# A transformer block on one core: the down product's tiles laid over the up operands in the order of their last reads, and its sums moved to VectorE

## The chip, the core and the metric

The kernel runs on one NeuronCore of a Trainium2 chip. Its engines work side by side from queues of their own: TensorE (PE) multiplies, VectorE (DVE), ScalarE (ACT) and GpSimd (POOL) do element-wise work, SyncE (SP) mostly issues DMA transfers. The metric is the device time of one execution in microseconds.

## The reference

One layer of a hybrid encoder, 1024 tokens by 1024 features in float32: two attentions, a gated merge, an output projection, and a feed-forward part. The change touches only the last part:

```python
    x = x + merged @ w_out[l]
    h2 = rms_norm(x, norm2[l])
    x = x + jnp.square(jax.nn.relu(h2 @ w_up[l])) @ w_down[l]
return rms_norm(x, final_norm)
```

`w_up` is 1024 x 4096, `w_down` 4096 x 1024.

## The kernel before

Every large product is a Strassen product of 2 x 2 blocks: seven block products in place of eight, named by their weight operand A11, S1, S2, S3, S4, A12, A22, each with an activation operand B11, T1, T2, T3, B22, B21, T4 (sums and differences of blocks). Each factor is split in a high and a low part (`wh`, `wl` of a weight, `xh`, `xl` of an operand), and each product is three matmuls: high by high, low by high, high by low. ACT casts the high part (L148 for weights, L251 for operands); the low part is a subtraction, on POOL for weights (L150) and on DVE for operands (L252).

*Up.* Sixteen units `u` run all seven products in the order A11, S2, S1, S3, A12, S4, A22, twelve matmuls each, with the seven operands held in SBUF in `xop`. DVE combines the banks (L481 to L493), applies relu and the norm (L820), ACT squares, and the results are stored as the seven operands of down in `a_dram`.

*Down.* The outer loop runs over the seven products in the order of `STEPS` (A11, S1, S2, S3, S4, A12, A22), the inner one over 16 steps `k`, with twelve matmuls a step into four PSUM banks `dA` or `dS`. `prepare` runs three steps ahead (`LEAD`): it loads an operand tile from `a_dram` (tile `xr`, transfers called xB or xT, six buffers), splits it (`xB11h`, `xT1l` and so on, four buffers each), and makes the weight. The weight tiles are `ka` (A11's, kept and turned into S3's in place, later loaded anew) and `ks` (S1's, then S2's, then S4's, in place), 16 each; quarters that are only passing are `wr`.

Sums: `p1`, `u`, `v`, `w` (in the profile `accp`, `accu`, `accv`, `accw`), four tiles of 128 x 512 each, gather the products. `evacuate` empties the four banks at the end of a product, `between` is a generator that is stepped once per step of the next product; `residual` loads a tile `r` of the layer's input to the feed-forward part and adds it; `final` squares and scales for the last norm.

Where tiles lie: pools are stacked from the left and the right end of SBUF. `operands` opens a pool for each named operand of up, 16 KB per partition each, on the left, and at the end of up they are closed, and down's pools take their place from the left on. A tile of down waits until the tile that lay there before has been read for the last time. The instructions of each engine are then put in order by a scheduler, so the text of the code gives dependencies and priorities and not the final order.

Of the kernel before, what the change touches and what calls it, by code (L numbers as in the profile page):

```python
# [14 lines left out]
ALU = mybir.AluOpType  # L15
# [56 lines left out]
def hs(h):  # L72
    return slice(h * HALF, (h + 1) * HALF)
# [3 lines left out]
def hybrid_block(ctx: ExitStack, tc: tile.TileContext, xT, g1, wall, wf, fb, relb, relt, rows, g2, g3, outT):  # L77
    nc = tc.nc
    V, A, G, T = nc.vector, nc.scalar, nc.gpsimd, nc.tensor
# [4 lines left out]
    def pool(stack, name, side, bufs=1, **kw):  # L84
        return stack.enter_context(tc.tile_pool(name=name, bufs=bufs, side=side, reuse_waits="tile", **kw))
# [9 lines left out]
    def tmp(name, dt=F32):  # L95
        return tp.tile([P, HALF], dt, tag="t", name=name, bufs=8)
# [9 lines left out]
    for n, (step, cm) in enumerate(((-1, 1), (1, -1))):  # L106
        m = cpool.tile([P, 3, P], F32R, tag=f"mask{n}", name=f"mask{n}")
# [180 lines left out]
    for h in range(2):  # L288
        banks = [psd[1 - h].tile([P, HALF], F32, tag="d", name=f"g{c}_{h}") for c in range(EARLY_GATES)]
# [423 lines left out]
    rest, steps = load_rest(*heads[0]), iter(())  # L713
    for n, hd in enumerate(heads):
        sk, more = rest, iter(())
        if n < 15:
            rest = load_rest(*heads[n + 1])
# [31 lines left out]
    for j in range(4):  # L749
        for h in range(2):  # L750
            t = tmp("olt")
            load(t, o_dram[j, :, hs(h)])
            split((oh[:, j, hs(h)], ol[:, j, hs(h)]), t, V)
    for c in range(8):
        for h in range(2):
            m = tmp("m")
# [10 lines left out]
    def operands(*keys):  # L767
        for n in keys:
            p = pool(hstack, "h" + n, "left")
            xop[n] = tuple(p.tile([P, 4, HALF], F32R, tag=n + s, name=n + s) for s in "hl")  # L770

    operands("B11", "B21")
    accs = accs2 = [rstd[:, hs(h)] for h in range(2)]
    held = {}
    for h in range(2):
        if h == 1:
            operands("T2", "T1", "T3", "B22", "T4")
        for n, c in enumerate(PAIRED):
            k = c % 4
            g = gt[:, 1, c:c + 1]  # L780
            w = plain_w(U_OUT + n // 2, n % 2)
            xr = tmp("xr2")
            load(xr, xT[:, c, hs(h)])
            ps = dense(psm[n % 2], f"o{c}_{h}", w, [(mop[h][0][:, kk, :], mop[h][1][:, kk, :]) for kk in range(KC)])
            V.tensor_tensor(xr, ps, xr, op=ALU.add)  # L785
            store(x2_dram[:, c, hs(h)], xr)
            sum_squares(xr, n == 0, accs[h], V if h else G)
            xg = tmp("xg")
            V.tensor_scalar(xg, xr, g, None, op0=ALU.mult)  # L789
            if h == 0:  # L790
                key = "B11" if c < 4 else "B21"
                split((xop[key][0][:, k, :], xop[key][1][:, k, :]), xg, V)
                continue
            old = tmp("xo")
            load(old, x2_dram[:, c, hs(0)])
            A.activation(old, old, AF.Copy, scale=g)
            held[c] = (old, xg)
            if c >= 4:
                split((xop["B22"][0][:, k, :], xop["B22"][1][:, k, :]), xg, V)
                combine(xop, k, *held[k], *held[c], (V, V))  # L800
        mstack[h].close()
# [39 lines left out]
    def sums(*names):  # L841
        p = pool(ctx, "acc" + names[0], "left")
        for n in names:
            acc[n] = p.tile([P, 4, HALF], F32, tag="acc" + n, name="acc" + n)

    held = {}
    sums("p1", "u")
    hp = {"a": pool(ctx, "ka", "left"), "s": pool(ctx, "ks", "left")}
    sums("v", "w")
    xr = pool(ctx, "xr", "right")  # L850

    def hold(t, k):
        held[t, k] = hp[t].tile([P, HALF], F32, tag=t, name=f"k{t}{k}", bufs=16)
# [23 lines left out]
    p1, au, av, aw = [acc[n] for n in ("p1", "u", "v", "w")]  # L877

    def residual(dst, m, row, h, src, eng):

        r = tmp(f"r{m}_{row}_{h}")
        load(r, x2_dram[:, m + 4 * row, hs(h)])
        eng.tensor_tensor(dst[:, m, :], src[:, m, :], r, op=ALU.add)

    def final(dst, m, row, h):

        dst = dst[:, m, :]
        sum_squares(dst, h not in begun, accs[h], V)
        begun.add(h)
        A.activation(dst, dst, AF.Copy, scale=gt[:, 2, m + 4 * row:m + 4 * row + 1])  # L890
# [17 lines left out]
                n += 1  # L908
                yield

    def evacuate(n, m, bank):
        at = lambda t: t[:, m, :]
        if n in ("A11", "S1"):
            A.copy(at({"A11": p1, "S1": av}[n]), bank)
        elif n == "S2":
            V.tensor_tensor(at(au), bank, at(p1), op=ALU.add)
        else:
            for t in {"S3": (aw, au), "S4": (av,), "A12": (p1,), "A22": (au,)}[n]:
                V.tensor_tensor(at(t), bank, at(t), op=ALU.add)

    def between(n):

        for m in range(4):
            at = lambda t: t[:, m, :]
            if n == "S2":
                V.tensor_tensor(at(av), at(av), at(au), op=ALU.add)
                residual(aw, m, 1, 1, av, V)
                yield
                residual(au, m, 1, 0, au, G)
            elif n == "S3":  # L930
                residual(av, m, 0, 1, av, G)
                yield
                final(aw, m, 1, 1)
            elif n == "S4":
                residual(p1, m, 0, 0, p1, G)
                final(av, m, 0, 1)
            elif n == "A12":
                final(p1, m, 0, 0)
            elif n == "A22":
                final(au, m, 1, 0)  # L940
            yield
        if n == "S4":
            yield
            yield from finish(psm[0], 1, (av, aw), (V, G))
        elif n == "A22":
            yield from finish(psm[1], 0, (p1, au), (V, V, G))
# [10 lines left out]
    ready, rest = [], iter(())  # L957
    for s, (i, n, x, k) in enumerate(steps):
        while len(ready) < min(s + LEAD + 1, len(steps)):
            ready.append(prepare(*steps[len(ready)][1:]))  # L960
        if k == 0:
            banks = [psm[i % 2].tile([P, HALF], F32, tag="d", name=f"d{n}_{m}") for m in range(4)]
        xs, wh, wl = ready[s]
        for m in range(4):
            product(banks[m], k == 0, [((wh[:, m, :], wl[:, m, :]), xs)], k < 15)
        if k:
            next(rest, None)
        if k == 15:
            for m in range(4):
                evacuate(n, m, banks[m])  # L970
            rest = between(n)
    for _ in rest:
        pass

# [61 lines left out]
```

## Time and profile before

| what | us |
|---|---|
| runs | 1597.46, 1597.52, 1600.31; median 1597.52 |
| profiled execution | 1596.17, its span 1594.4, mean granted clock 0.969 |
| TensorE busy | 1476.5 (93%) |
| DVE, ACT, POOL busy | 1051.9 (66%), 741.5 (47%), 964.5 (60%) |
| up's last matmul to down's first, from the span's start | 1240.1 to 1257.2 |
| down's seven products | 1257.2 to 1574.9 |
| after the last matmul of down | some 20 |

In a group's row the numbers are the count, then durations in ns. In a timeline's row they are the start and the duration in us, then the engine, the line, the operation, output and inputs, and in brackets how long the engine had been idle before it and what ended that. SPq is SyncE's queue of transfers. In a row of waits: total, times, longest.

### The profile page before, as it was taken

To read this page: it belongs to the slowest core of one execution; us is meant where nothing else is said; L and a number is where in the kernel's file an instruction comes from. 1 tells how busy PE (TensorE), PEld (TensorE's weight loads), DVE (VectorE), ACT (ScalarE), POOL (GpSimd) and SP (SyncE) were. 2 spreads that over 40 slices of the span, in tenths; PEclk is the share of its full clock that TensorE was granted. 3 is DMA by queue.
4 is the path that set the end of the run, shared out by engine and by line. 5 is a ranking of instruction groups with operands and counts; after the bars stand their busy time and mean duration, and the time that the engine had idled before them with its cause. 6 is when DMAs were issued, how large, how long until landed. Compare 5 with 4: busy or idle time off the path is not lost.

```text
span 1594.4 us, 21236 instructions
## 1 busy us (share of the span) xinstructions
PE 1476.5 (93%) x6788; PEld 1213.0 (76%) x6788; DVE 1051.9 (66%) x1552; ACT 741.5 (47%) x1391; POOL 964.5 (60%) x746
## 2 busy tenths in 40 slices
PE   6798999999979899999999879999999599989996
PEld 4586888888858788888777758888888488868885
DVE  8988555644457687765414887666666588677763
ACT  5543333343348787657324544333333344435552
POOL 6886777778742232111199648888886355466661
PEclk9899999999979999999999979999999799999998
DMA  4155666873487878874566544444445965444371
GB/s 152 48 146 138 189 195 200 219 206 121 163 192 169 175 161 206 206 204 108 193 210 197 187 145 165 159 151 154 151 152 173 336 218 165 129 142 132 115 226 56
DMA packets 154288, 269.21 MB, mean 169 GB/s; under 512 B 22264, under 2 KB 39928, under 8 KB 151040
## 3 DMA queue, kind: packets, MB, share of 16 engines
q1 hardware_dynamic: 82880, 149.37, 31.3%
q10 hardware_dynamic: 50304, 84.24, 16.5%
q0 software_dynamic: 20992, 34.25, 9.9%
q8 instruction: 53, 0.87, 0.2%
q14 instruction: 59, 0.48, 0.1%
HBM read 181.48 MB, written 86.31 MB: 168 GB/s over the span
## 4 chain that ended last, share of the span: by engine, by line
PE 36%; DMA 6%; DVE 5%; issue 2%; POOL 1%; ACT 1%; SPq 0%; ACTq 0%; DVEq 0%; POOLq 0%
PE u L201 18%; PE dS L201 9%; PE dA L201 6%; DMA wr<-wall 2%; PE o L201 1%; DMA ka<-wall 1%; PE m L201 1%; DMA olt<-o_dram 1%; DMA xr<-xT 1%; POOL wl L150 0%; POOL ml L252 0%; POOL m L759 0%; DVE xr L785 0%; DVE xg L789 0%; DVE ks L866 0%
## 5 line engine op out<-in xcount | busy, mean ns | idle before, releaser
L150 POOL TENSOR_TENSOR wl_A<-wr,wh_A 128x512 fp32r<-128x512 f32 x121 | 174.6, 1447 | 64.1 <-ACT wh_A L148 54.8
L150 POOL TENSOR_TENSOR wl_S<-S,wh_S 128x512 fp32r<-128x512 f32 x105 | 153.0, 1461 | 33.0 <-ACT wh_S L148 30.9
L148 ACT CAST wh_A<-wr 128x512 fp32r<-128x512 f32 x121 | 75.0, 620 | 116.7 <-DMA a_dram<-at 28.1
L252 DVE TENSOR_TENSOR tl<-p,th 128x512 fp32r<-128x512 f32 (+1 forms) x192 | 108.6, 587 | 28.6 <-ACT th L251 23.7
L150 POOL TENSOR_TENSOR wl_S<-ks,wh_S 128x512 fp32r<-128x512 f32 x48 | 68.7, 1434 | 56.1 <-ACT wh_S L148 53.6
L251 ACT CAST th<-p 128x512 fp32r<-128x512 f32 (+1 forms) x192 | 92.4, 509 | 10.3 <-PE pv L676 4.4
L434 DVE CUSTOM_DVE_ANT_0 s<-s,bc 128x384 f32<-128x384 f32 (+3 forms) x128 | 69.7, 562 | 38.5 <-PE s L427 24.1
L148 ACT CAST wh_S<-S 128x512 fp32r<-128x512 f32 x105 | 63.8, 618 | 63.7 <-POOL S L173 27.2
L493 DVE TENSOR_TENSOR cc<-u,u 128x512 f32<-128x512 f32 x70 | 48.0, 686 | 61.1 <-PE u L201 61.0
L427 PE MATMUL s<-qk 128*128 128x384 f32 (+2 forms) x192 | 63.1, 362 | 22.7 <-DMA qk<-qk_dram 15.4
L171 POOL TENSOR_TENSOR S<-wr,wr 128x512 f32<-128x512 f32 x36 | 51.5, 1432 | 53.0 <-DMA wr<-wall 46.7
L150 POOL TENSOR_TENSOR wl_A<-ka,wh_A 128x512 fp32r<-128x512 f32 x32 | 45.6, 1431 | 53.1 <-ACT wh_A L148 53.1
L821 ACT ACTIVATE v<-v 128x512 f32<-128x512 f32 x64 | 40.4, 631 | 69.3 <-DVE v L820 69.1
L660 PE MATMUL st<-sk 82*128 82x512 f32 (+1 forms) x192 | 66.1, 345 | 2.1 <-DMA sk<-m_rows 2.1
L652 PE MATMUL st<-qk 128*128 128x512 f32 (+1 forms) x192 | 66.6, 351 | 0.6 <-ACT p L672 0.5
L675 PE MATMUL pv<-th,v 128*128 128x512 f32 (+1 forms) x192 | 65.6, 342 | 1.0 <-ACT on L688 0.6
L677 PE MATMUL pv<-tl,v 128*128 128x512 f32 (+1 forms) x192 | 65.0, 339 | 0.1
L676 PE MATMUL pv<-th,v 128*64 128x512 f32 (+1 forms) x192 | 64.7, 337 | 0.0
L672 ACT ACTIVATE p<-st,ncq 128x512 f32<-128x512 f32 (+1 forms) x96 | 54.3, 598 | 22.1 <-PE st L668 15.5
L251 ACT CAST qkh<-qk 128x512 fp32r<-128x512 f32 x32 | 19.9, 622 | 95.2 <-DMA qk_dram<-qkl 46.0
L148 ACT CAST wh_S<-ks 128x512 fp32r<-128x512 f32 x48 | 29.8, 621 | 67.8 <-PE dS L201 59.4
L427 PEld LDWEIGHTS s<-qk 128*128 128x128 f32 x192 | 36.2, 199 | 31.4 <-DMA qk<-qk_dram 8.8
(369 smaller groups left out, 5180.4 us busy)
## 6 DMA issues: line engine op xcount, KB each, us to landing
wr<-wall SPq DMA_DIRECT2D x259, 256.0 KB
qk<-qk_dram POOLq DMA_DIRECT2D x16, 1024.0 KB, 6.3
a_dram<-at ACTq DMA_DIRECT2D x64, 256.0 KB
xT<-a_dram SPq DMA_DIRECT2D x64, 256.0 KB
qk_dram<-qkh ACTq DMA_DIRECT2D x96, 128.0 KB
a_dram<-v ACTq DMA_DIRECT2D x48, 256.0 KB
xB<-a_dram SPq DMA_DIRECT2D x48, 256.0 KB
z_dram<-zt ACTq DMA_DIRECT2D x32, 256.0 KB
```

Source lines behind the costliest of these rows:

```text
L148: A.copy(wh, src)
L150: G.tensor_tensor(wl, src, wh.bitcast(F32), op=ALU.subtract)
L201: T.matmul(bank, w[wi], x[xi], start=(first and t == 0), stop=(t == n - 1 and not part), skip_group_check=part or not first)
L251: A.copy(dst[0], src)
L252: eng.tensor_tensor(dst[1], src, dst[0].bitcast(F32), op=ALU.subtract)
L427: T.matmul(ps[:, :n], qk[:, 1, i * P:(i + 1) * P], qk[:, 0, ks:ks + n], start=True, stop=not diag)
L434: V.tensor_tensor_reduce(ps[:, :v], ps[:, :v], bc[:, b0:b0 + v], 1.0, prev, ALU.add, ALU.min, out)
L652: T.matmul(ps[:, c], qk[:, 0, keys], qk[:, 1, qs], start=True, stop=False)
L660: T.matmul(ps[:, c], sk[:, 0, keys], sk[:, 1, qs], start=False, stop=not extra)
L675: T.matmul(pv[:, c], v3[hh][:, j, 1:3, :], th[:, c], start=first, stop=False)
L676: T.matmul(pv[0:HD, c], v3[hh][:, j, 0, :], th[:, c], start=False, stop=False)
L677: T.matmul(pv[:, c], v3[hh][:, j, 1:3, :], tl[:, c], start=False, stop=last)
```

## The change

Three edits.

1. Up's operands are laid out from the left as B11, T2, T1, T3, B21, B22, T4, the order in which a unit reads them (before: B11, B21, T2, T1, T3, B22, T4). Five pools are now opened before the first half of the output projection and two before the second; before it was two and five.
2. Down's pools take their place as `xq` (split operands), `xr` (raw operands), `ka`, the sums `p1` and `u`, `ks`, the sums `v` and `w`, all on the left. Before it was `xq`, `p1` and `u`, `ka`, `ks`, `v` and `w`, with `xr` on the right, where up's epilogue tiles had been. So `xq` lies over B11 in both; `xr` now lies over T2, `ka` over T2 to T3 and `ks` over B21 to T4.
3. `evacuate` is gone. `between` reads the banks itself, one instruction or two per step, and all residuals are on DVE. The grouping of the sums is another one: residuals of `u`, `w` and `v` are added after S1 (with A11's sum added to `v`), `p1`'s after S2, and S2's bank is then added to `u`, `v` and `w` straight from PSUM. Before, `u` took S2's bank, `v` took `u`, and `w` took `v` with its residual. The loop runs out a generator that is left over at a product's end before it starts the next.

```diff
-    operands("B11", "B21")
+    operands("B11", "T2", "T1", "T3", "B21")
...
         if h == 1:
-            operands("T2", "T1", "T3", "B22", "T4")
+            operands("B22", "T4")
...
+    xr = pool(ctx, "xr", "left")
+    hp = {"a": pool(ctx, "ka", "left")}
     sums("p1", "u")
-    hp = {"a": pool(ctx, "ka", "left"), "s": pool(ctx, "ks", "left")}
+    hp["s"] = pool(ctx, "ks", "left")
     sums("v", "w")
-    xr = pool(ctx, "xr", "right")
...
-    def evacuate(n, m, bank):
-        at = lambda t: t[:, m, :]
-        if n in ("A11", "S1"):
-            A.copy(at({"A11": p1, "S1": av}[n]), bank)
-        elif n == "S2":
-            V.tensor_tensor(at(au), bank, at(p1), op=ALU.add)
-        else:
-            for t in {"S3": (aw, au), "S4": (av,), "A12": (p1,), "A22": (au,)}[n]:
-                V.tensor_tensor(at(t), bank, at(t), op=ALU.add)
-
-    def between(n):
+    def between(n, banks):
 
         for m in range(4):
             at = lambda t: t[:, m, :]
-            if n == "S2":
-                V.tensor_tensor(at(av), at(av), at(au), op=ALU.add)
+            add = lambda t, src: V.tensor_tensor(at(t), src, at(t), op=ALU.add)
+            bank = banks[m]
+            if n == "A11":
+                A.copy(at(p1), bank)
+            elif n == "S1":
+                A.copy(at(av), bank)
+                residual(au, m, 1, 0, p1, V)
+                yield
+                add(av, at(p1))
+                yield
                 residual(aw, m, 1, 1, av, V)
                 yield
-                residual(au, m, 1, 0, au, G)
+                residual(av, m, 0, 1, av, V)
+            elif n == "S2":
+                for t in (au, av, aw):
+                    add(t, bank)
+                    yield
+                residual(p1, m, 0, 0, p1, V)
             elif n == "S3":
-                residual(av, m, 0, 1, av, G)
+                add(aw, bank)
+                yield
+                add(au, bank)
                 yield
                 final(aw, m, 1, 1)
-            elif n == "S4":
-                residual(p1, m, 0, 0, p1, G)
-                final(av, m, 0, 1)
...
+            else:
+                t, row, h = {"S4": (av, 0, 1), "A12": (p1, 0, 0), "A22": (au, 1, 0)}[n]
+                add(t, bank)
+                final(t, m, row, h)
...
         if k == 15:
-            for m in range(4):
-                evacuate(n, m, banks[m])
-            rest = between(n)
+            for _ in rest:
+                pass
+            rest = between(n, banks)
```

How the scheduled instructions move, at three places.

SP's queue at the change from up to down. `wr` are weight quarters, `ka` down's first weights, `xB` its first operand tiles (the number tells tiles apart). Before, from the last of 16 ka transfers on:

```order
L860 DMA ka_12701<-wall 128x512
L143 DMA wr_3_12782<-wall 128x512
L143 DMA wr_2_12784<-wall 128x512
L143 DMA wr_3_12814<-wall 128x512
L143 DMA wr_2_12816<-wall 128x512
L143 DMA wr_3_12846<-wall 128x512
L143 DMA wr_2_12848<-wall 128x512
L143 DMA wr_3_12874<-wall 128x512
L143 DMA wr_2_12876<-wall 128x512
L950 DMA xB_12367<-a_dram 128x512
L950 DMA xB_12379<-a_dram 128x512
```

The same queue now, from the last of up's rows on:

```order
L143 DMA wr_2_12756<-wall 128x512
L953 DMA xB_12367<-a_dram 128x512
L953 DMA xB_12379<-a_dram 128x512
L953 DMA xB_12391<-a_dram 128x512
L953 DMA xB_12403<-a_dram 128x512
L953 DMA xB_12431<-a_dram 128x512
L953 DMA xB_12455<-a_dram 128x512
L953 DMA xB_12479<-a_dram 128x512
L953 DMA xB_12503<-a_dram 128x512
L861 DMA ka_12373<-wall 128x512
L861 DMA ka_12385<-wall 128x512
```

Eight operand tiles moved from behind the 16 ka and 8 wr to ahead of them.

DVE at the start of S2 (operand T2). Before, from S1's last rows on:

```order
L870 TENSOR_TENSOR ka_12701<-ka_12701,wr_3_13968 128x512
L252 TENSOR_TENSOR xT1l_13122<-xT_13119,xT1h_13121 128x512
L252 TENSOR_TENSOR xT1l_13150<-xT_13147,xT1h_13149 128x512
L252 TENSOR_TENSOR xT2l_13178<-xT_13175,xT2h_13177 128x512
L252 TENSOR_TENSOR xT2l_13201<-xT_13198,xT2h_13200 128x512
L252 TENSOR_TENSOR xT2l_13224<-xT_13221,xT2h_13223 128x512
L252 TENSOR_TENSOR xT2l_13251<-xT_13248,xT2h_13250 128x512
```

The same place now, from the third low part on:

```order
L252 TENSOR_TENSOR xT2l_13224<-xT_13221,xT2h_13223 128x512
L916 TENSOR_TENSOR accv<-accp_12357,accv 128x512 x2
L884 TENSOR_TENSOR accw<-accv,r_1_1_13345 128x512
L916 TENSOR_TENSOR accv<-accp_12357,accv 128x512
L884 TENSOR_TENSOR accw<-accv,r_1_1_13448 128x512
L884 TENSOR_TENSOR accv<-accv,r_0_1_13371 128x512
L252 TENSOR_TENSOR xT2l_13247<-xT_13244,xT2h_13246 128x512
L916 TENSOR_TENSOR accv<-accp_12357,accv 128x512
L884 TENSOR_TENSOR accw<-accv,r_1_1_13551 128x512
L884 TENSOR_TENSOR accv<-accv,r_0_1_13474 128x512
L884 TENSOR_TENSOR accp_12357<-accp_12357,r_0_0_13798 128x512
L252 TENSOR_TENSOR xT2l_13274<-xT_13271,xT2h_13273 128x512
```

Where S2's low parts had followed each other, additions of two SBUF tiles now stand between the third and the fourth, the fourth and the fifth, and so on to the seventh (4, then 2, after these rows).

DVE at the start of S3 (operand T3), as S2's banks `dS` are emptied. Before:

```order
L873 TENSOR_TENSOR ks_12781<-ka_14043,ks_12781 128x512
L916 TENSOR_TENSOR accu<-dS_0_13259,accp_12351 128x512
L252 TENSOR_TENSOR xT3l_13604<-xT_13601,xT3h_13603 128x512
L916 TENSOR_TENSOR accu<-dS_1_13260,accp_12351 128x512
L926 TENSOR_TENSOR accv<-accv,accu 128x512
L873 TENSOR_TENSOR ks_12813<-ka_14076,ks_12813 128x512
L916 TENSOR_TENSOR accu<-dS_2_13261,accp_12351 128x512
L916 TENSOR_TENSOR accu<-dS_3_13262,accp_12351 128x512
L926 TENSOR_TENSOR accv<-accv,accu 128x512
L883 TENSOR_TENSOR accw<-accv,r_1_1_13685 128x512
L252 TENSOR_TENSOR xT3l_13633<-xT_13630,xT3h_13632 128x512
```

Now, from the third low part (`xT3l`) to the fourth:

```order
L252 TENSOR_TENSOR xT3l_13638<-xT_13635,xT3h_13637 128x512
L916 TENSOR_TENSOR accu<-dS_1_13256,accu 128x512
L916 TENSOR_TENSOR accv<-dS_1_13256,accv 128x512
L916 TENSOR_TENSOR accw<-dS_1_13256,accw 128x512
L874 TENSOR_TENSOR ks_12809<-ka_14100,ks_12809 128x512
L916 TENSOR_TENSOR accu<-dS_2_13257,accu 128x512
L916 TENSOR_TENSOR accv<-dS_2_13257,accv 128x512
L916 TENSOR_TENSOR accw<-dS_2_13257,accw 128x512
L916 TENSOR_TENSOR accu<-dS_3_13258,accu 128x512
L916 TENSOR_TENSOR accv<-dS_3_13258,accv 128x512
L916 TENSOR_TENSOR accw<-dS_3_13258,accw 128x512
L252 TENSOR_TENSOR xT3l_13669<-xT_13666,xT3h_13668 128x512
```

The three additions of bank 0 stand ahead of these rows. Every addition here now reads a bank; those of two SBUF tiles (L926, L883) have left the place.

More of the change, by code (lines that the diff above doesn't have):

```diff
@@ L909, in finish @@
                 yield
-    def evacuate(n, m, bank):
-        at = lambda t: t[:, m, :]
-        if n in ("A11", "S1"):
-            A.copy(at({"A11": p1, "S1": av}[n]), bank)
-        elif n == "S2":
-            V.tensor_tensor(at(au), bank, at(p1), op=ALU.add)
-        else:
-            for t in {"S3": (aw, au), "S4": (av,), "A12": (p1,), "A22": (au,)}[n]:
-                V.tensor_tensor(at(t), bank, at(t), op=ALU.add)
-    def between(n):
+    def between(n, banks):
         for m in range(4):
             at = lambda t: t[:, m, :]
-            if n == "S2":
-                V.tensor_tensor(at(av), at(av), at(au), op=ALU.add)
+            add = lambda t, src: V.tensor_tensor(at(t), src, at(t), op=ALU.add)
[8 more added lines that the diff above has]
+                yield
                 residual(aw, m, 1, 1, av, V)
                 yield
-                residual(au, m, 1, 0, au, G)
+                residual(av, m, 0, 1, av, V)
[4 more added lines that the diff above has]
+                residual(p1, m, 0, 0, p1, V)
             elif n == "S3":
-                residual(av, m, 0, 1, av, G)
+                add(aw, bank)
+                yield
+                add(au, bank)
                 yield
                 final(aw, m, 1, 1)
-            elif n == "S4":
-                residual(p1, m, 0, 0, p1, G)
-                final(av, m, 0, 1)
[L937 to L940, printed above, removed]
+            else:
+                t, row, h = {"S4": (av, 0, 1), "A12": (p1, 0, 0), "A22": (au, 1, 0)}[n]
+                add(t, bank)
+                final(t, m, row, h)
             yield
```

## The prediction

> **What bounds the kernel now.** I first read the busy time stage by stage, cut at the seven products of the down matmul (from, to; PE; PEld; DVE; ACT; POOL; clock; DMA share; GB/s).
>
> ```profile
> 1257.20:1302.90 45.70, 45.50 (x192) 37.21 (x193) 31.33 (x36) 20.24 (x36) 21.16 (x15) 0.96 0.80 263
> 1302.90:1347.20 44.30, 44.30 (x193) 35.70 (x192) 42.91 (x42) 20.16 (x37) 23.27 (x17) 1.00 0.56 175
> 1347.20:1390.90 43.70, 43.70 (x194) 36.19 (x194) 23.33 (x20) 19.05 (x34) 20.68 (x16) 1.00 0.40 121
> 1390.90:1443.90 53.00, 46.41 (x193) 37.48 (x192) 42.72 (x44) 18.97 (x34) 33.37 (x22) 0.94 0.51 153
> 1443.90:1487.60 43.70, 43.70 (x195) 36.18 (x194) 30.50 (x28) 23.13 (x41) 27.88 (x19) 1.00 0.41 120
> 1487.60:1531.10 43.50, 43.50 (x201) 36.22 (x200) 31.84 (x33) 22.31 (x41) 32.77 (x22) 1.00 0.54 170
> 1531.10:1574.90 43.80, 43.80 (x194) 36.25 (x194) 21.98 (x22) 18.86 (x33) 15.78 (x12) 1.00 0.35 109
> ```
>
> They are A11, S1, S2, S3, S4, A12, A22. TensorE alone needs 43.7 for a product, 2.72 for each of its 16 steps; three products take just that. A11 is 2.0 over, S1 0.6, S3 9.3. Then the waits of TensorE, and its rows at the three holes:
>
> ```profile
> PE dA L201 <- ACT xB11h L251: 16.8, 1, 16.8
> PE dS L201 <- DVE xT3l L252: 6.6, 2, 3.7
> 1240.09 0.39 PE L201 MATMUL u<-T4h,wl_A 128*128 128x512 f32 x1
> 1257.24 2.07 PE L201 MATMUL dA<-xB11h,wh_A 128*128 128x512 f32 x4 [16.76 <-ACT xB11h L251]
> 1405.86 0.50 PE L201 MATMUL dS<-xT3l,wh_S 128*128 128x512 f32 x1 [2.92 <-DVE xT3l L252]
> 1406.20 0.40 PE L201 MATMUL dS<-xT3h,wl_S 128*128 128x512 f32 x1
> 1412.58 0.80 PE L201 MATMUL dS<-xT3l,wh_S 128*128 128x512 f32 x1 [3.67 <-DVE xT3l L252]
> 1413.60 0.63 PE L201 MATMUL dS<-xT3l,wh_S 128*128 128x512 f32 x1
> ```
>
> Up's last matmul and down's first lie 16.8 us apart; within S3 DVE is late twice. After each long hole matmuls take 0.63 instead of 0.39: the rest of A11's and S3's excess. Why down starts late is in the queue of transfers and in the first weight and operand:
>
> ```profile
> 1227.28 0.33 SPq L143 DMA_DIRECT2D wr<-wall  x1
> 1227.70 12.97 SPq L860 DMA_DIRECT2D ka<-wall  x16
> 1241.39 9.12 SPq L143 DMA_DIRECT2D wr<-wall  x8
> 1250.61 4.24 SPq L950 DMA_DIRECT2D xB<-a_dram  x6
> 1232.37 0.62 ACT L148 CAST wh_A<-ka 128x512 fp32r<-128x512 f32 x1 [4.62 <-DMA a_dram<-at]
> 1233.07 1.30 POOL L150 TENSOR_TENSOR wl_A<-ka,wh_A 128x512 fp32r<-128x512 f32 x1 [5.81 <-ACT wh_A L148]
> 1256.57 2.65 ACT L251 CAST xB11h<-xB 128x512 fp32r<-128x512 f32 x4 [9.90 <-DMA xB<-a_dram]
> ```
>
> The weights were split at 1234.4, but the operand's transfer stood behind 24 others and was issued 22.9 us after the first of them. That is order, not bandwidth.
>
> **The start of down.** `xr` now lies over T2, which is read for the last time when the last unit's S2 product ends: one product (2.72) ahead of the end of its S1, which this row shows at 1229.6, so at 1226.9.
>
> ```profile
> 1229.64 0.69 DVE L483 TENSOR_TENSOR c<-u,u 128x512 f32<-128x512 f32 x1 [1.17 <-PE u L201]
> 1231.26 6.30 DMA ka<-wall
> ```
>
> So the eight xB transfers start at 1227.7. `xr` has six buffers: the first six go out 0.42 apart, the seventh waits for the first split on DVE. From issue to split weight start it was 4.7 for the first ka (1227.70 to 1232.37), 6.3 for a later one. First xB there at 1232.4, cast 0.62, DVE 0.68: seventh and eighth leave at 1233.7 and 1234.4, the first ka about 1235. It lands in 4.7 to 6.3, is cast and split (0.62 and 1.3): 1241.6 to 1243.2. Up's matmuls end at 1240.5, so 1 to 3 us of hole remain; I take 2, and 0.3 for a cool clock, since after the 2.92 hole only one matmul was much longer. Weight k must be there 2.72 k later, while ka transfers left every 0.81 (12.97 over 16): the first hole does not repeat. What A11 had over (2.0) goes with the hole. Term: 16.8 + 2.0 − 2.3 = **−16.5** (−11 if the ka come 5 later, −18.8 if nothing is left).
>
> **The sums, now on DVE.** Counted in the code, the change takes 12 residuals off POOL and gives DVE 20 instructions; in all, DVE's additions of two SBUF tiles go from 8 to 20, those with a PSUM bank from 24 to 32. The prices (min/median/max ns):
>
> ```profile
> L252 DVE TENSOR_TENSOR xT1l<-xT,xT1h x16: 677/679/1786, 1297.6 to 1342.0; 128x512 fp32r<-128x512 f32 x16
> L883 DVE TENSOR_TENSOR accw<-accv,r x4: 679/1756/1774, 1396.1 to 1409.1; 128x512 f32<-128x512 f32 x4
> L919 DVE TENSOR_TENSOR accw<-dS,accw x4: 678/680/692, 1442.4 to 1446.6; 128x512 f32<-128x512 f32 x4
> L883 POOL TENSOR_TENSOR accv<-accv,r x4: 1312/1736/1742, 1399.6 to 1451.9; 128x512 f32<-128x512 f32 x4
> 1303.41 0.68 DVE L252 TENSOR_TENSOR xT1l<-xT,xT1h 128x512 fp32r<-128x512 f32 x1
> 1341.38 1.28 DVE L252 TENSOR_TENSOR xT1l<-xT,xT1h 128x512 fp32r<-128x512 f32 x2
> ```
>
> An addition from PSUM always takes 0.68 (0.60 from start to start), one of two SBUF tiles 0.68 or 1.7. In S1 DVE never rests (42.9 of 44.3): from the third xT1l (1303.41) to the end of the sixteenth (1342.66) it does 38 instructions in 39.25 us, 1.03 each, with POOL doing one split a step. 38 × 0.61 is 23.2; the other 16 over 14 POOL splits is 1.1 for each. So DVE alone pays 0.61 an addition, and once 1.1 for each POOL split beside it.
>
> The Trainium skill speaks against the move here: SBUF — State Buffer, section Who interferes with whom, says that a DVE instruction with two SBUF inputs contends with a GpSimd one that reads SBUF, and one with at most one SBUF input does not. The L883, L252 and L919 rows agree. By that rule the 12 moved residuals become exposed, though the 12 POOL instructions that they would have met are gone too; it gives the same sum as the rows.
>
> S1: in the new DVE order 47 instructions stand from the first residual to the sixteenth xT1l (seven late sums of `ks` and four residuals of `au` more than before). It can't begin before A11's banks are copied, so about at S1's start: 39.25 + 9 × 0.61 + 1.1 for one more split = 45.8 after it. TensorE wants the sixteenth at 15 × 2.72 + 0.2 = 41.0. That is 4.8 late; a few of its rows precede the copies, so I take 4.5, S1 48.2: **+3.9** (0 to +6).
>
> S2 used to leave DVE 20 us idle. Now its 16 additions stand almost in one block between the third and the seventh xT2l: six, xT2l, four, xT2l, four, xT2l, two, xT2l. S1's last operand is ready just as TensorE takes it, 2.5 before S2's start, so the third xT2l is done at 0.6 after it (3 × 1.03); at 1.03 each the fifth is done at 13.0 and wanted at 11.1, the sixth at 18.1 against 13.8, the seventh at 21.2 against 16.5: 4.7 late at most. While TensorE waits, POOL gets no new weights, and the additions cost 0.61: **+3.5** (0 to +6).
>
> S3: the rows that made it late, and the four between them:
>
> ```profile
> 1390.75 0.68 DVE L916 TENSOR_TENSOR accu<-dS,accp 128x512 f32<-128x512 f32 x1
> 1396.66 1.78 DVE L252 TENSOR_TENSOR xT3l<-xT,xT3h 128x512 fp32r<-128x512 f32 x1
> 1402.37 1.77 DVE L883 TENSOR_TENSOR accw<-accv,r 128x512 f32<-128x512 f32 x1
> 1404.06 1.75 DVE L252 TENSOR_TENSOR xT3l<-xT,xT3h 128x512 fp32r<-128x512 f32 x1
> 1410.78 1.74 DVE L252 TENSOR_TENSOR xT3l<-xT,xT3h 128x512 fp32r<-128x512 f32 x1
> ```
>
> POOL's residuals and weight splits met every SBUF addition. Now no residual lies here on either engine; 12 PSUM additions follow S2's end, with one xT3l and one `ks` between them. From 0.24 before S3's start: 12 × 0.6 + 3 × 0.61 up to the fourth xT3l = 9.0, with one or two splits met 10.1 to 11.2, so done 8.8 to 11.0 after the start. TensorE wants it at 8.2, and has 0.9 of other matmuls that its order puts ahead: 0 to 2 late, then two instructions a step (1.2 + 1.1 = 2.3) recover. So the burst of evacuations is not dealt out, only made of cheap ones. Excess 1.5 instead of 9.3: **−7.8** (−9.3 to −3).
>
> S4, A12 and A22 ran at TensorE's pace and keep their DVE order; POOL's eight residuals less there are worth 0, as is the tail after 1575 with the same rows. The out stage keeps TensorE's order word for word: 0, unless B21's new place makes a cast wait, for which no row speaks.
>
> Sum: −16.5 + 3.9 + 3.5 − 7.8 = −16.9. The profiled execution took 1596.17 (span 1594.4, 1.8 around it), so 1579.3; it lay 1.35 below the median 1597.52, so on the scale of the runs **1580.5**.
>
> **Rivals.**
> - DVE keeps up: no new lateness in S1 and S2, S3 at 43.7: for it the operands' lead of three steps (8.2 us); against it DVE's 42.9 of 44.3 in S1. 1597.5 − 16.5 − 0.6 − 9.3 = 1571.
> - Lateness moves: S1 +5, S2 +5, S3 as late as it was less its 2.7 of slow clock, and such a slow stretch (2.7) in S2. For it S3's two holes, against it that PSUM additions don't collide. −16.5 + 5 + 5 − 2.7 + 2.7 = −6.5: 1591. TensorE: Matmul & The Clock Gate of the Trainium skill, section HAM oscillation, puts the drop at holes above some 3.4 us; the rows agree (2.92: one slow matmul, 3.67: a slow stretch), and by it holes of 1 to 2 would cost no clock.
> - Weights become the late operand: the ka behind eight xB land 5 to 7 later than I take, since SP stands at the seventh xB. Start −10.5 with its slow clock; sum −10.9: 1586.6.
> - Slower: if each SBUF addition paid the full 1.7, S1's 47 took 80 us, +36 on a product, over the 24.3 gained. It decides from 15 collisions beyond one per split, since 16.9 / 1.1 = 15. Against it, S1 has just one per split.
>
> **How the numbers follow.** Main case 0.52 (1575 to 1585), DVE keeps up 0.18, lateness moves 0.13, weights late 0.11, slower 0.02, nothing measurable 0.04. The range 1571 to 1590 leaves out the last two and most of the far ends of the first and third. Within 0.2% (3.2 us) this kernel's runs can't tell from no change. Faster 0.94, same 0.04, slower 0.02.
>
> **What would show it.** The first xB issued near 1228 and TensorE's hole before down 0 to 3 us; S1 and S2 near 48 and 47 with waits on xT1l and xT2l and DVE above 90% in both; S3 near 45. Wrong if down's first matmul waits for a weight beyond 5 us, if S1 and S2 stay at 43.7 (then the sum is too small), or if their lateness exceeds 6 each.

## The result, and the profile after

The changed kernel took 1587.99 us, the median of four runs (1584.89 to 1589.0, whose own median is 1586.97, and one of 1840.06 at a mean granted clock of 0.746 that the ratio leaves out); the kernel before took 1597.49. The ratio is 0.993, with a 95% interval of 0.9909 to 0.9952: faster, by 9.5 us where 17 had been forecast. The profiled execution took 1584.89, its span 1583.1 against 1594.4 before.

The changed kernel's busy time by stage, cut at the first matmuls of A11, S1, S2, S3 and S4 by their operands (columns as before), and TensorE's waits for its operands in down:

```profile
1240.70:1287.80 47.10, 44.88 (x192) 35.89 (x193) 32.01 (x32) 22.63 (x40) 30.76 (x21) 1.00 0.87 295
1287.80:1342.40 54.60, 48.31 (x193) 36.16 (x192) 50.50 (x59) 20.21 (x37) 23.61 (x16) 0.97 0.76 246
1342.40:1388.10 45.70, 44.47 (x194) 35.82 (x194) 35.48 (x35) 18.82 (x34) 23.20 (x16) 1.00 0.43 135
1388.10:1432.20 44.10, 43.78 (x193) 35.96 (x192) 36.53 (x44) 19.31 (x34) 21.92 (x16) 1.00 0.55 172
```

```profile
PE dS L201 <- DVE xT1l L252: 6.3, 5, 3.4
PE dA L201 <- DVE xB11l L252: 1.8, 3, 0.9
PE dS L201 <- DVE xT2l L252: 1.2, 3, 0.6
PE dS L201 <- DVE xT3l L252: 0.3, 1, 0.3
```

Cut in this way, an undisturbed product takes 43.5 (192 matmuls, 0.227 apart) and not the 43.7 of the prediction, whose cuts in the kernel before lie up to 0.4 early. The last two lie some 2 early: A12, with other matmuls between its own, takes 45.4, and down's last matmul ends at 1576.9 and not at 1574.9. S3 is down to 44.1 from 53.3, and the 16.8 us wait for `xB11h` is gone from the list. In their place S1 has 11.1 too much: 6.3 in which TensorE stood (54.60 less 48.31), and 4.8 in which its matmuls took longer than those 43.5. Two rows of TensorE's timeline show the new start of down and the longest hole in S1, and three of SP's queue show why down starts early:

```profile
1240.67 0.50 PE L201 MATMUL dA<-xB11h,wh_A 128*128 128x512 f32 x1 [0.19 <-ACT wh_A L148]
...
1300.98 0.50 PE L201 MATMUL dS<-xT1l,wh_S 128*128 128x512 f32 x1 [3.44 <-DVE xT1l L252]
```

```profile
1227.68 7.83 SPq L953 DMA_DIRECT2D xB<-a_dram  x8
1235.57 4.82 SPq L861 DMA_DIRECT2D ka<-wall  x8
...
1251.97 2.95 SPq L143 DMA_DIRECT2D wr<-wall  x3
```

The operands now go out at 1227.68, ahead of the weights. Before, the quarters `wr` for S1's weights went out between 1241.39 and 1250.5, ahead of the operands; three of them now leave as late as 1252 to 1255. That is what the rest of this text is about.

From span to span: start of down −16.6, A11 +1.2, S1 +10.2, S2 +2.2, S3 −9.2, the last three products 0, the tail after the last matmul's end +0.8 (18.3 against 17.5): −11.4, where the spans differ by 11.3.

### The profile page after: what moved, and what is told of

Its sections match the earlier page's. It is cut to its first block, busy times and chain, and to the rows that moved or that the text cites. A ratio compares the mean times of both kernels' runs of the same rounds, so it can differ in the third digit from the quotient of the medians.

```text
span 1583.1 us, 21213 instructions
## 1 busy us (share of the span) xinstructions
PE 1482.2 (94%) x6788; PEld 1212.9 (77%) x6788; DVE 1059.7 (67%) x1572; ACT 741.5 (47%) x1391; POOL 942.2 (60%) x734
## 4 chain that ended last, share of the span: by engine, by line
PE 36%; DVE 6%; DMA 5%; issue 2%; POOL 1%; ACT 1%; SPq 0%; DVEq 0%; ACTq 0%; POOLq 0%
PE u L201 17%; PE dS L201 8%; PE dA L201 5%; PE o L201 4%; DMA wr<-wall 2%; PE m L201 1%; DMA ka<-wall 1%; DVE ka L871 1%; DMA olt<-o_dram 1%; DMA xB<-a_dram 1%; DVE ks L867 1%; POOL ml L252 0%; DMA xr<-xT 0%; POOL m L759 0%; POOL wl L150 0%
## 5 line engine op out<-in xcount | busy, mean ns | idle before, releaser
L150 POOL TENSOR_TENSOR wl_A<-ka,wh_A 128x512 fp32r<-128x512 f32 x32 | 45.9, 1447 | 43.7 <-ACT wh_A L148 43.7
L672 ACT ACTIVATE p<-st,ncq 128x512 f32<-128x512 f32 (+1 forms) x96 | 54.1, 598 | 21.6 <-PE st L668 15.4
```

Source lines behind the costliest of these rows:

```text
L150: G.tensor_tensor(wl, src, wh.bitcast(F32), op=ALU.subtract)
```

## The experiments

Two theories stood at first for S1. A: S1's own weight sums (`ks`, L866, now L867) come late, since their quarters go round four buffers `wr`, and they stand in DVE's queue ahead of S1's operands. B: the residuals that are now on DVE in S1 lengthen it. The first four kernels share one set of runs of the kernel before (median 1598.34), jit3 to after_again another (1600.9), late_u_wr8 to all3 a third (1600.92), and spread16 has its own (1600.22); each ratio is to its set. In the table the products are from first matmul to first matmul in the profiled execution, to 0.1 us, and each is one profile of its kernel. Two profiles of the same code, changed and after_again, differ by 0.2 in A11 and S1, by 0.1 in S2 and by 1.4 in S3, so a difference of that size in S3 shows nothing.

| kernel | A11 | S1 | S2 | S3 | sum of the four | median us | ratio to before, 95% interval |
|---|---|---|---|---|---|---|---|
| before | 45.9 | 44.4 | 43.5 | 53.3 | 187.1 | 1597.49 | |
| changed | 47.1 | 54.6 | 45.7 | 44.1 | 191.5 | 1587.99 | 0.993 (0.9909 to 0.9952) |
| layout | 46.2 | 54.7 | 43.6 | 53.6 | 198.1 | 1594.19 | 0.9973 (0.9962 to 0.9985) |
| sums | 45.8 | 46.2 | 45.6 | 44.2 | 181.8 | 1595.56 | 0.9972 (0.9957 to 0.9988) |
| wr8 | 44.0 | 53.7 | 45.6 | 44.1 | 187.4 | 1581.83 | 0.9894 (0.9875 to 0.9913) |
| late_u | 47.0 | 54.6 | 43.6 | 45.4 | 190.6 | 1586.4 | 0.993 (0.991 to 0.9951) |
| jit3 | 46.4 | 51.4 | 45.7 | 45.3 | 188.8 | 1585.38 | 0.9915 (0.9884 to 0.9947) |
| jit3_wr6 | 45.0 | 49.3 | 45.7 | 49.8 | 189.8 | 1585.14 | 0.9905 (0.9883 to 0.9927) |
| ka_pool | 48.2 | 54.3 | 53.4 | 44.1 | 200.0 | 1596.23 | 0.9979 (0.9963 to 0.9995) |
| after_again | 46.9 | 54.4 | 45.6 | 45.5 | 192.4 | 1589.09 | 0.9926 (0.9907 to 0.9946) |
| late_u_wr8 | 44.4 | 52.6 | 43.7 | 45.3 | 186.0 | 1580.52 | 0.988 (0.9852 to 0.9907) |
| late_u_jit3 | 46.4 | 50.4 | 43.6 | 47.5 | 187.9 | 1584.31 | 0.9897 (0.9876 to 0.9919) |
| all3 | 44.1 | 47.2 | 43.6 | 51.0 | 185.9 | 1579.26 | 0.988 (0.9854 to 0.9907) |
| spread16 | 43.8 | 46.6 | 55.4 | 45.4 | 191.2 | 1587.22 | 0.9921 (0.9891 to 0.995) |

One caution for reading it: up's last matmul is at 1240.1 in the changed kernel and at 1243.7 in the second profile of the same code (after_again), and over all the profiles at 1239.0 to 1252.9. Most of this is there before up: the first matmul of the output projection (`o`) starts at 817.3, 819.8, and 814.4 to 830.1. So the products are compared here, and the totals only by their ratios.

**layout: edits 1 and 2 alone.** The sums stay as before.

```diff
-    operands("B11", "B21")
+    operands("B11", "T2", "T1", "T3", "B21")
...
+    xr = pool(ctx, "xr", "left")
+    hp = {"a": pool(ctx, "ka", "left")}
     sums("p1", "u")
```

> Only the two layout edits; the sums, their order and POOL's residuals are those of before. Both theories: the hole ahead of down closes (17 us become less than 1), and S3 stays near 53 us, as it was before. Theory A (S1 is late because the sums of ks now stand in DVE's queue between the operands of S1, each waiting for its two wr transfers): S1 takes 49 to 52 us although no residual is in it, total 1586 to 1590. Theory B (S1 is late because of the four residuals of u that were moved to DVE): S1 is back at 44 to 45 us, total 1580 to 1583.

Its stages S1 and S3, and what DVE waited for from 1240 to 1345:

```profile
1292.40:1347.10 54.70, 48.40 (x193) 36.14 (x192) 46.39 (x54) 20.14 (x37) 22.27 (x16) 0.97 0.71 226
...
1390.70:1444.30 53.60, 48.25 (x193) 37.87 (x192) 43.67 (x44) 19.09 (x34) 34.87 (x22) 0.94 0.47 144
```

```profile
DVE ks L867 <- DMA wr<-wall: 10.7, 9, 2.2
```

S1 is as long as in the changed kernel with no residual in it. Theory B falls as the cause by itself: S1's length comes with the layout. But S1 is also 2.7 above theory A's 49 to 52, and the time 4 us above A's, so A is not the whole of it. S3 keeps the excess that it had before.

**sums: edit 3 alone.** The layout stays as before; `between` and the residuals are the changed kernel's.

> Only the third edit (sums from the banks, residuals on DVE), with the layout of before. Both theories: the 16.8 us hole ahead of down stays, S2 is 1 to 2 us longer, and S3 falls from 53 to about 44. Theory A: S1 is 45 to 47 us (four additions more than before, the sums of ks are done by then), total 1590 to 1593. Theory B: S1 is 52 to 55 us, total 1597 to 1600.

Its S1 and S3:

```profile
1301.50:1347.70 46.20, 45.99 (x193) 35.16 (x192) 44.85 (x47) 20.22 (x37) 22.06 (x16) 1.00 0.62 192
...
1393.30:1437.50 44.20, 43.89 (x194) 35.97 (x193) 36.79 (x45) 19.38 (x34) 21.95 (x16) 1.00 0.55 171
```

The residuals and sums alone make S1 1.8 longer, S2 2.1, and S3 9.1 shorter. S1 is where theory A had it and not at B's 52 to 55; the time is 2.6 above A's and below B's. So S3's gain belongs to edit 3, the start to edits 1 and 2, and each part alone is worth about as much as the other (0.9973 and 0.9972).

**wr8: eight buffers of their own for down's passing quarters.**

```diff
+    wq = pool(ctx, "wq", "left")
+    def passing(u, n):
+        q = wq.tile([P, HALF], F32, tag="wq", name=f"wq{u}_{n}", bufs=8)
...
-            V.tensor_tensor(hold("s", k), quarter(u, 3), quarter(u, 2), op=ALU.add)
+            V.tensor_tensor(hold("s", k), passing(u, 3), passing(u, 2), op=ALU.add)
```

> The changed kernel with eight buffers of their own for down's passing weight quarters in place of four shared with up. Theory A (the wait is the round trip of a pair of transfers through four buffers): DVE's waits for wr (10 us in the changed kernel up to S1's end) go to under 3 us, S1 falls from 54.6 to 47 to 49, total 1579 to 1582. Theory B (residuals and DVE's load): S1 stays at 53 to 55, total 1585 to 1589. If it is bandwidth that makes the sums late, and not the number of buffers, the waits stay too.

Its A11 and S1:

```profile
1241.30:1285.30 44.00, 43.89 (x194) 35.94 (x192) 32.20 (x32) 22.28 (x41) 30.84 (x21) 1.00 0.98 341
1285.30:1339.00 53.70, 46.76 (x194) 36.65 (x193) 51.38 (x60) 20.20 (x37) 32.89 (x16) 0.97 0.79 264
```

The transfers run closer (share 0.98 against 0.87) and A11 loses 3.1 of the 3.6 that it had over 43.5, so these were theory A's. S1 hardly moves and stays where theory B had it, though the time is theory A's; here DVE is busy for 51.4 of S1's 53.7, and up to S1's end it waits 5.4 for quarters where it had waited 10.0. Theory A as it stood falls for S1 too: with quarters sooner, DVE has nearly all of S1 to work.

**late_u: u's residual after S3 instead of in S1.** (The code writes it behind S1's last step, but it needs only A11's sum, and the scheduler puts it into S1.)

```diff
-                residual(au, m, 1, 0, p1, V)
...
-                for t in (au, av, aw):
+                V.tensor_tensor(at(au), bank, at(p1), op=ALU.add)
...
+                residual(au, m, 1, 0, au, V)
```

> The changed kernel, except that u takes S2's bank with A11's sum as before and its residual is added after S3, so that no residual stands in S1 and three fewer additions of two SBUF tiles in S2. Theory A: S1 is 50 to 52 us (the waits for wr stay), total 1582 to 1585. Theory B: S1 is 44 to 46 us, total 1576 to 1579.

S1 stays at 54.6, above what either theory gave, and S2 comes down to 43.6; S3's 45.4 is that of after_again. Moving the residual makes no difference in S1 while the quarters are late, and the time moves by less than its interval.

What DVE does in S1 says what was missing. These are its groups there, of the changed kernel first, of the kernel before below (count, busy us, mean ns, idle before):

```profile
L871 DVE TENSOR_TENSOR ka<-ka,wr 128x512 f32<-128x512 f32 x16 | 19.0, 1209 | 0.7 <-DMA wr<-wall 0.5
L869 DVE TENSOR_TENSOR ks<-ks,ka 128x512 f32<-128x512 f32 x14 | 11.7, 836 | 0.0
L252 DVE TENSOR_TENSOR xT1l<-xT,xT1h 128x512 fp32r<-128x512 f32 x16 | 10.8, 680 | 0.0
L867 DVE TENSOR_TENSOR ks<-wr,wr 128x512 f32<-128x512 f32 x5 | 4.8, 957 | 2.4 <-DMA wr<-wall 2.4
...
L884 DVE TENSOR_TENSOR accu<-accp,r 128x512 f32<-128x512 f32 x4 | 3.7, 949 | 0.0
```

```profile
L870 DVE TENSOR_TENSOR ka<-ka,wr 128x512 f32<-128x512 f32 x13 | 16.0, 1230 | 0.4
L252 DVE TENSOR_TENSOR xT1l<-xT,xT1h 128x512 fp32r<-128x512 f32 x14 | 13.9, 995 | 0.0
L868 DVE TENSOR_TENSOR ks<-ks,ka 128x512 f32<-128x512 f32 x12 | 12.6, 1046 | 0.0
```

The largest group in both is L871 (L870 before): S3's weights, two products ahead of their use. Before, they filled S1 to the brim (DVE busy for 42.9 of 44.3), and S1's sums had been done by A11's end. So there was a third theory, "queue": three things stand ahead of S1's operands on DVE, the sums that wait for quarters, u's residuals and S3's subtractions, and the next one takes over when one is removed.

**jit3: S3's weights into four buffers of their own.** A subtraction must then wait until an earlier one's weight has been split, so 12 of the 16 leave S1.

```diff
-            V.tensor_tensor(held["a", k], held["a", k], quarter(u, 3), op=ALU.subtract)
+            d = k3.tile([P, HALF], F32, tag="k3", name=f"k3{k}", bufs=4)
+            V.tensor_tensor(d, held["a", k], quarter(u, 3), op=ALU.subtract)
```

> The changed kernel, with S3's weights made into a tag k3 of its own with four buffers instead of in place over A11's: 12 of the 16 subtractions that stood on DVE in S1 (19.0 us for the 16) move into S2, and the loads of their quarters with them. Theory 'queue': S1 is long because DVE has more to do in it than TensorE (16 operands, 7 sums of S1, 14 subtractions for S2, 16 for S3: 50.5 us busy plus 2.4 us of waits for quarters, against 43.7). Then S1 falls from 54.6 to 47 to 50 (the late sums at its start remain), S2 is 44 to 46 with what moved into it, and the time is 1580 to 1584. Theory 'arrival': S1 is long only because its first sums get their quarters late. Those come ahead of S3's in the queue, so S1 stays at 53 to 55 and the time at 1586 to 1590.

S1 came to 51.4, between what the two theories gave: DVE has 43.9 to do there in place of 50.5 and waits 10.8 for quarters in A11 and S1.

**jit3_wr6: jit3 with six buffers for the quarters.**

> As the run before, and down's passing quarters in six buffers of their own, so that S1's sums get their quarters sooner. Theory 'queue': with eight such buffers alone S1 stayed at 53.7 while DVE stood idle for nothing between its first operand and its third; with S3's subtractions gone as well, S1 is 44 to 46, A11 44 to 45, and the time is 1572 to 1578, the sum of the two effects or more. Theory 'arrival': S1 stays above 50, and the time stands at the 1581.8 of the eight buffers alone.

Its S1 and S3, and the longest hole of TensorE in each:

```profile
1284.70:1334.00 49.30, 45.94 (x193) 36.88 (x192) 45.62 (x52) 20.20 (x37) 28.96 (x16) 0.97 0.72 242
...
1379.70:1429.50 49.80, 45.55 (x194) 36.95 (x193) 40.72 (x52) 19.36 (x34) 23.29 (x16) 0.97 0.61 192
```

```profile
1297.16 0.50 PE L201 MATMUL dS<-xT1l,wh_S 128*128 128x512 f32 x1 [3.36 <-DVE xT1l L252]
...
1393.52 0.79 PE L201 MATMUL dS<-xT3l,wh_S 128*128 128x512 f32 x1 [3.87 <-DVE xT3l L252]
```

A miss by 7 us from the upper end of what was expected, of which some 3 go with the set of runs (its kernel before took 1600.9, against 1597.49). S1 fell less than expected: one hole is left in it, and on DVE ahead of that `xT1l` three of u's residuals stand between sums. And what was pushed out of S1 came down in S3, beside S2's twelve bank additions.

**ka_pool: S3's subtractions on POOL, in their old places.**

```diff
-            V.tensor_tensor(held["a", k], held["a", k], quarter(u, 3), op=ALU.subtract)
+            G.tensor_tensor(held["a", k], held["a", k], quarter(u, 3), op=ALU.subtract)
```

> The changed kernel with S3's 16 subtractions on POOL instead of DVE, at the same places in time. The loads stay where they are. Theory 'queue': DVE loses up to 19 us in S1, POOL gains 16 instructions (some 1.2 to 2 us each beside its 32 us), DVE's remaining two-input adds pay more for the shared side; S1 46 to 50, time 1578 to 1584. Theory 'arrival': S1 53 to 55, time 1586 to 1590.

DVE's two largest groups in S1, and the hole that S2 has now:

```profile
L252 DVE TENSOR_TENSOR xT1l<-xT,xT1h 128x512 fp32r<-128x512 f32 x16 | 21.7, 1363 | 0.0
L869 DVE TENSOR_TENSOR ks<-ks,ka 128x512 f32<-128x512 f32 x14 | 18.3, 1305 | 4.8 <-POOL wl_S L150 4.8
```

```profile
1360.18 0.80 PE L201 MATMUL dS<-xT2l,wh_S 128*128 128x512 f32 x1 [6.15 <-DVE xT2l L252]
```

Both theories missed the time (1596.23). DVE got rid of 19.0 us of work, but the same `xT1l` cost 21.7 in place of 10.8 and the same L869 18.3 in place of 11.7, beside more instructions of POOL; its busy time in S1 fell by only 4.6, from 50.5 to 45.9, and it now waits 4.8 there for POOL. S1 stays at 54.3, which theory 'arrival' had too, and S2 gets a hole. So this run does not tell the two theories apart; it shows that handing this work to POOL does not help.

**after_again: the changed kernel itself beside these three.**

> The changed kernel again, on the chip of the three others. Both theories: S1 54 to 55, A11 47, the time 1586 to 1590 and the ratio to the kernel before 0.991 to 0.995.

All as expected: S1 54.4, ratio 0.9926. What it adds is S3's 45.5 for 44.1.

**late_u_wr8, late_u_jit3 and all3: the edits two by two, and all three** (all3 has six buffers for the quarters, late_u_wr8 eight).

> The changed kernel with u's residual moved behind S3 and eight own buffers for down's passing quarters; S3's subtractions stay on DVE in S1. Theory 'one queue, three loads': the late quarters, u's four residuals and S3's 16 subtractions all stand ahead of S1's operands on DVE, and taking one away only uncovers the next. With sums early and no residual, only the 16 subtractions are left: S1 is 49 to 52 (from 53.7 with eight buffers alone), A11 44, S2 43.6, time 1576 to 1581. Rival 'arrival of the quarters alone': the residuals never mattered, S1 stays at 53.7 and the time at about 1580 (2 less for S2).

> The changed kernel with u's residual moved behind S3 and S3's subtractions into four buffers of their own (so 12 of them leave S1); the quarters pass through the four old buffers. Theory 'one queue, three loads': the sums still wait for their quarters, so the residuals' place goes to waiting: S1 stays at 49 to 52, as with the subtractions moved alone (51.4), S3 grows by what moved into it (45 to 49), time 1582 to 1588. Rival 'the residuals set the 3.4 us hole': that hole goes, S1 46 to 48.

> The changed kernel with all three: u's residual behind S3, six own buffers for the passing quarters, S3's subtractions in four buffers of their own. Theory 'one queue, three loads': nothing is left in S1 that TensorE would wait for, S1 is 44 to 46 (from 54.6), A11 45, S2 43.6, but S3 has 12 subtractions, S2's sums and residuals to do and is 46 to 50; time 1570 to 1577. Rival 'arrival alone': S1 stays at the 49.3 of buffers and subtractions without the residuals moved. Rival 'DVE slower of itself' (its two-input adds beside POOL's): S1 stays over 50.

S1 of late_u_jit3 and of all3, and all3's S3:

```profile
1288.40:1338.80 50.40, 46.77 (x194) 36.58 (x193) 41.10 (x47) 20.29 (x38) 22.51 (x16) 0.97 0.66 205
```

```profile
1285.10:1332.30 47.20, 45.21 (x194) 35.50 (x193) 44.01 (x48) 20.21 (x37) 26.00 (x16) 1.00 0.71 230
...
1375.90:1426.90 51.00, 46.31 (x193) 37.48 (x192) 43.17 (x56) 19.33 (x34) 25.56 (x16) 0.93 0.61 188
```

S1 by what is removed: nothing 54.6; u's residual 54.6; quarters earlier 53.7; S3's subtractions 51.4; residual and quarters 52.6; residual and subtractions 50.4; quarters and subtractions 49.3; all three 47.2. The residual is worth 0 alone, 1.1 with earlier quarters, 1.0 with the subtractions gone and 2.1 with both. That fits one queue with three loads. Part of the last 2.1 is TensorE's clock: jit3_wr6 has a hole of 3.36 in S1 and behind it seven matmuls that leave 0.2 late each, 1.4 together, while in all3 the longest hole there is 1.05 and none follow. Of these kernels only all3 comes within 3.7 of TensorE's time (44 to 46 had been expected: a miss of 1.2). late_u_wr8's S1 lies 0.6 above the 49 to 52 expected, between that and the rival's 53.7. But all3 pays in S3 (51.0, beyond the 46 to 50 expected), and its time of 1579.26 is some 2 above what had been expected.

**spread16: late_u_wr8, with S3's subtractions one per step at S2's steps.** Their quarters come through the ring of the raw operands.

```diff
-LEAD, XB, XR = 3, 4, 6
+LEAD, XB, XR = 3, 4, 8
...
+    def third(k):
+        q = xr.tile([P, HALF], F32, tag="xr", name=f"q3_{k}", bufs=XR)
+        load(q, wall[U_DOWN + k, :, 3, :])
+        V.tensor_tensor(held["a", k], held["a", k], q, op=ALU.subtract)
...
         elif n == "S2":
             V.tensor_tensor(held["s", k], held["s", k], held["a", k], op=ALU.subtract)
+            if k < 16:
+                third(k)
```

> The changed kernel with u's residual behind S3, eight own buffers for S1's passing quarters, and S3's 16 subtractions written at S2's steps, their quarters loaded through the raw operands' ring (eight buffers instead of six), so that they come one per step: 8 in S1, 8 in S2, none in S3. Theory 'one queue, three loads, and their spacing': DVE's busy time in S1 falls from 49.9 (without the spacing) to some 42.5 of 43.7 and in S2 rises from 33.2 to 40.6, both under TensorE's time; S1 44 to 46, S2 43.6 to 45, S3 44 to 46, A11 44 to 45, time 1570 to 1575. Rival 'DVE is full over the four products and only passes its lateness on': what leaves S1 comes back in S2 or S3, the four products together stay at the 186 of the kernel with three things removed, time 1578 to 1582.

S1 and S2, and what DVE waited for:

```profile
1288.00:1334.60 46.60, 45.37 (x194) 35.48 (x192) 36.27 (x41) 20.43 (x37) 25.15 (x16) 1.00 0.67 218
1334.60:1390.00 55.40, 48.54 (x193) 38.86 (x192) 37.84 (x45) 18.76 (x34) 22.42 (x16) 0.91 0.57 183
```

```profile
DVE ka L866 <- DMA q<-wall: 22.5, 15, 3.5
```

S1 came out at 46.6, 0.6 above the 44 to 46 forecast and 6.0 below late_u_wr8's, which says once more that S3's subtractions held it up (five of the 16 are left in S1; the two more buffers for raw operands came with it and were not tried alone). S2 did not come out as forecast: DVE has only 37.8 of 55.4 to do there, but the subtractions now wait 22.5 us in all for their quarters, 14.9 of it in S2, and S2's operands queue behind them. The quarters leave late: between 1300 and 1395 SP's issue of them waits 14.5 for an earlier quarter and 7.1 for DVE's use of one. Both theories' times are missed (1587.22). It is the fault of the changed kernel's S1 once more, made by hand.

late_u_wr8 and all3, both at 0.988, have the lowest ratios, clear of the kernel before; against the changed kernel their intervals only just part (upper end 0.9907, where its two sets begin at 0.9909 and 0.9907). late_u_wr8 needs only two small edits.

## Why the prediction was right in sign and 7.5 us off

Of the 7.5 us, 5.6 show in the profiles (1584.89 for 1579.3): S1 6.3 more than forecast, start of down with A11 1.1 and the tail 0.8 more, S2 1.3 and S3 1.4 less. The rest is the spread between a profiled run and the median.

**The start of down: the mechanism right, the size 1.1 off.** The term of −16.5 is for the hole and A11's excess together, and these gave −15.4: −16.6 for the hole and +1.2 for A11. The operands go out at 1227.68 (1227.7 forecast) and a hole of 0.2 is left where 2 had been allowed. What failed here is "What A11 had over (2.0) goes with the hole": the slow clock did go, but A11 is now 3.6 over, most of which eight buffers for the quarters take away. The two misses go against each other; that the hole alone comes so near −16.5 is chance.

**S1: the term that was mis-sized, +10.2 measured for +3.9.** The step that failed is "It can't begin before A11's banks are copied, so about at S1's start". The DVE rows of the changed kernel, S1 beginning at 1287.80:

```profile
1289.24 1.15 DVE L867 TENSOR_TENSOR ks<-wr,wr 128x512 f32<-128x512 f32 x1 [0.63 <-DMA wr<-wall]
...
1292.14 1.12 DVE L867 TENSOR_TENSOR ks<-wr,wr 128x512 f32<-128x512 f32 x1 [1.14 <-DMA wr<-wall]
...
1295.10 1.14 DVE L867 TENSOR_TENSOR ks<-wr,wr 128x512 f32<-128x512 f32 x1 [0.63 <-DMA wr<-wall]
1296.16 0.68 DVE L884 TENSOR_TENSOR accu<-accp,r 128x512 f32<-128x512 f32 x1
...
1297.37 2.35 DVE L884 TENSOR_TENSOR accu<-accp,r 128x512 f32<-128x512 f32 x2
1299.64 0.68 DVE L867 TENSOR_TENSOR ks<-wr,wr 128x512 f32<-128x512 f32 x1
1300.24 0.68 DVE L252 TENSOR_TENSOR xT1l<-xT,xT1h 128x512 fp32r<-128x512 f32 x1
...
1301.57 0.69 DVE L867 TENSOR_TENSOR ks<-wr,wr 128x512 f32<-128x512 f32 x1
...
1336.36 1.28 DVE L252 TENSOR_TENSOR xT1l<-xT,xT1h 128x512 fp32r<-128x512 f32 x2
```

The first residual starts at 1296.16, 8.4 after S1's start: seven instructions stand ahead of it there, and three of them are sums that each wait for a transfer. From there to the end of the last `xT1l` (1337.64) it takes 41.5, less than the 45.8 counted. The count of 47 instructions held, and so did the price (47 × 0.61, and 1.1 for each of the 11 POOL splits that fall into it, are 40.8), but a count of DVE's work says nothing while DVE waits. The last sum of `ks` in the kernel before is this one:

```profile
1288.24 0.69 DVE L866 TENSOR_TENSOR ks<-wr,wr 128x512 f32<-128x512 f32 x1 [2.08 <-DMA wr<-wall]
```

It was done 14.2 before S1's first matmul (1303.1). In the changed kernel S1 starts 15.3 earlier, and the last sum ends 13.3 later, at 1302.26, 14.5 after S1's start. Six of the 16 sums were done by A11's start in the kernel before, none in the changed one, and five are made in S1. The prediction counted seven late sums behind the first residual (with the four residuals that is 11, though its sum adds 9) and priced them as work; two stand there. It didn't ask when their quarters come, though it had read that the quarters' transfers were put behind the operands'. The gain at the start was bought with S1's lead.

By the prediction's own signs this step was wrong, since S1's lateness is beyond 6; DVE was to be over 90% busy in S1 and S2, and was 92% and 78%. It also took the lengthening for edit 3's. The runs show it to be the layout's (54.7 alone), with edit 3 alone at +1.8.

**S2: right, +2.2 for +3.5.** It is the residuals' doing: 43.6 in layout, which has none there, 45.6 in sums. TensorE's three waits for `xT2l` are at most 0.6 long, where 4.7 had been counted as the latest.

**S3: right, −9.2 for −7.8.** The twelve additions from PSUM at its start cost one wait of 0.3; the excess of 1.5 that was allowed is 0.6, and 2.0 in after_again. sums has the gain alone.

**The tail** was put at 0 and took 0.8 more. In the fourteen profiles it is 17.5 to 18.3, 17.5 also in jit3_wr6 and spread16, which have edit 3 too; no run looked into it.

**The rivals.** By the time alone, "Weights become the late operand" (1586.6) fits better than the main case. It is excluded by its mechanism: down's first matmul waited 0.19 for a weight, where weights 5 to 7 later were needed. "Lateness moves" did not happen in S2 and S3 of the changed kernel, but it is what the experiments ran into as soon as work was taken out of S1 (S3 at 49.8 and 51.0, S2 at 55.4). "DVE keeps up" holds for S2 and S3 only.

What stays open: why all3 still has 3.7 too much in S1 (its DVE is busy for 44.0 of 47.2), S3's 1.4 between two profiles of one code, and what spreads the time at which up ends.

## What to carry to other kernels

When a stage is made to start earlier, ask of everything that was prepared in the wait ahead of it, not only of its first operand, when it arrives now: here the 16 sums for S1 had a lead of 14 us from the hole that was closed, and S1 lost 10 of the 16.6 us won. A count of an engine's instructions bounds a stage only where each has its inputs; look for the instruction in the queue that waits for a transfer, since whatever stands behind it is late with it. And where one queue carries several loads that are each late, removing one shows nothing or moves the hole: try them together before a cause is dismissed.

## What the runs showed of the hardware

Behind some of TensorE's holes in S1 to S3 its matmuls leave 0.43 apart in place of 0.23 for some 3 us, beginning up to 1.6 after the hole's end; the granted clock was 0.65 from 1301 to 1304 in the changed kernel, behind its hole of 3.44. Such a stretch followed every hole from 3.36 us up, and none of up to 1.6. Between these, of holes with no other as long just ahead, it goes both ways: 2.06 and 2.80 (late_u_jit3), 2.20 (spread16), 2.34 (ka_pool), 2.74 (late_u_wr8) and 2.81 (late_u) were followed by one, 2.77 (wr8) and 2.80 (layout) were not, and S3's hole of 2.92 was in layout but not in the kernel before. Here are late_u_jit3 and, below, wr8:

```profile
1393.69 0.50 PE L201 MATMUL dS<-xT3l,wh_S 128*128 128x512 f32 x1 [2.06 <-DVE xT3l L252]
...
1395.00 0.63 PE L201 MATMUL dS<-xT3l,wh_S 128*128 128x512 f32 x1
```

```profile
1297.62 0.50 PE L201 MATMUL dS<-xT1l,wh_S 128*128 128x512 f32 x1 [2.77 <-DVE xT1l L252]
1297.96 0.40 PE L201 MATMUL dS<-xT1h,wl_S 128*128 128x512 f32 x1
```

The prediction took from TensorE: Matmul & The Clock Gate of the Trainium skill, section HAM oscillation, that the clock drops at holes above some 3.4 us, and found its rows in agreement. The runs don't bear that out as a limit of a single hole: one of 2 us can cost a clock drop on top, some seven matmuls that each leave 0.2 late.

That DVE's additions of two SBUF tiles pay for POOL's instructions beside them was known ahead; ka_pool shows how much: 16 subtractions fewer on DVE in S1, 14 of them run by POOL there in 22.4 us, and DVE's busy time went down by 4.6 where the kernel had shown 19.0 for them.
